# A two-layer hybrid diffusion step on one core: the start of the slots woven into the last features, RWKV factors taken off GpSimd

## The chip, the core and the metric

The kernel runs on 1 core of one Trainium2 chip. The metric is the device time of one execution in microseconds (us). TensorE does the matrix products, VectorE, ScalarE and GpSimd the elementwise work, and SyncE (SP) issues every DMA. All arithmetic is fp32; most products run as three passes over operands split into a high and a low part ("mm3").

## What is computed

Two layers work on 1152 tokens: 1024 latent ones and 128 of a prompt. Cut to what matters here, a layer of the reference is:

```python
u = layer_norm(x) * (1.0 + scale) + shift                    # adaLN from the conditioning
r, k, v, g, cq, ckv, kr, gm, xl, gl = split_in(u @ w_in)     # "features": columns of w_in
y_rw, S_fin = rwkv_branch(u, r, k, v, g, S0, l, P)           # scan over tokens, both directions
y_mla = block_attention(qn, qr, kn, kr_all, vv) * silu(gm)   # 8 heads, softmax over 1152 keys
y_lru, h_fin = lru_branch(xl, gl, h0, l, P)
x = layer_norm(ALPHA * x + gate * (concat(y_rw, y_mla, y_lru) @ w_out))

# a step of the RWKV scan, per head of 64
sa = S @ (-kk_t);  S = S * w_t + sa (x) (kk_t * a_t) + v_t (x) k_t;  y = S @ r_t
```

The latent tokens read the prompt's cached context, the prompt's tokens only themselves, so their attention is over 128 keys (no more than one tile).

## The kernel before

**Stages of a layer.** First come values, rope keys and latents of all tokens (token tiles of 128), then the queries, then 16 "features": column tiles of 128 of the input projection, each over three blocks of 384 tokens (24 matmuls a block). The loop over `n_` walks them in `order`. Weights of three features are loaded and split at a time. Other work is hung on the loop: a piece of the next adaLN per feature (`adaln_piece`), the LRU scan (`lru_piece`, features 3 to 8) and the RWKV factors (`rwkv_tile`, `RW_AT`: two token tiles at each of features 9 to 12 and the last at 13, nine in all). The last three features are taken by token block instead: feature step 13 does block 0 of all three, 14 block 1, 15 block 2.

**RWKV factors.** For each tile of 128 tokens and each direction d, `rwkv_tile` makes four factors from the summed log decay Lc: z = exp(Lc - lw) times the negated normalised key, r = exp(Lc) times the receptance, b and k from exp(-Lc). `gtt` is GpSimd's tensor_tensor, `vtt`, `vts` and `vstt` are VectorE's, `act` and `sca_` ScalarE's. The normalised key `nkk` lies in a tile of tag `mxb`, of which there is one; the results lie in tags `abz` and `ls`, two each, and go to DRAM (`zr_d`, `bk_d`).

**Values and slots.** `value(i)` makes the attention values of key tile i (ten of them, the tenth is the prompt's). After that the layer runs 48 slots, three for each unit of one head and 512 queries. A slot has named blocks (A0, G, A1, B, C, S) in which queued work is hung: queries are loaded (`load_q`) and split (`split_q`, the subtraction on GpSimd) some slots ahead, the row maxima of the scores are found (`max_q` for four query tiles over 1024 keys, `max_last` for the rest, `max_rows` puts them into the query), heads' keys are made (`keys`), and the RWKV chunks are taken through their products (`win_load`, `win_products`, `win_transposes`), the inversion of a triangular matrix (`inv_load`, `inv_blocks16` on GpSimd, `inv_store`) and the scan. Work of negative slots is what the slots begin from: the first head's keys, the first units' maxima, the first chunks' products. All maxima use the one PSUM tile of tag `b`.

**The prompt's attention** (two units `ups` of four heads) is done before the slots: `prompt_keys`, `max_last`, `max_rows`, `scores`, `values`, `sums`, then `finish` (reciprocals of the sums, through DRAM and back to be spread over partitions) and `gate`. Both take their queries in `qs_`, the tiles that the first units use too.

**Order.** The Tile framework orders the instructions of each engine by priority (the order in which they are written) and readiness, and gives out the tiles. The prompt and the negative slots are written after all values, in a block with a raised priority:

```python
        with tc.high_priority(offset=tc.cur_priority - p_late):
            value(9)
            ...
            for g, u in enumerate(ups):
                prompt_keys(g)
                max_last(u)
                ...
            for slot in range(min(s for s, _ in todo), 0):
                for b in ("A0", "G", "A1", "B", "C", "S"):
                    run(slot, b)
```

Large tiles come from tag `t`, ten buffers: the normalised tokens `Ub` (six, two for each block), weights, keys, the values V0 and V1, and the tiles `sets`, `s3`, `s4`, `s5` of the RWKV chunks (`s5` holds the inversion's X and U_).

## Time and profile before

| | |
|---|---|
| three runs, median (lowest, highest) | 2005.73 us (2003.27, 2010.9) |
| profiled execution | 2003.78 us, span of its instructions 2001.9 us |
| TensorE busy / mean granted clock | 1815.0 us / 0.944 |
| VectorE, ScalarE, GpSimd busy | 1202.3, 924.4, 684.7 us |

In the views, PE is TensorE, PEld its weight loads, DVE VectorE, ACT ScalarE, POOL GpSimd. "busy, mean ns" of a group is the summed time and the mean of one instruction; "idle before <- releaser" is the time in which the engine stood idle just before it, and what it waited for. PEclk is the granted TensorE clock as a share of 2.4 GHz. L121, L116 are the helpers through which the matmuls and the VectorE and ScalarE instructions are issued. Stages are at these times: RWKV factors begin in layer 0 at 336.57 us and in layer 1 at 1342.10, slot 0's scores at 511.47 and 1491.04.

### The profile page before, as it was taken

To read this page: it belongs to the slowest core of one execution; us is meant where nothing else is said; L and a number is where in the kernel's file an instruction comes from. 1 tells how busy PE (TensorE), PEld (TensorE's weight loads), DVE (VectorE), ACT (ScalarE), POOL (GpSimd) and SP (SyncE) were. 2 spreads that over 40 slices of the span, in tenths; PEclk is the share of its full clock that TensorE was granted. 3 is DMA by queue.
4 is the path that set the end of the run, shared out by engine and by line. 5 is a ranking of instruction groups with operands and counts; after the bars stand their busy time and mean duration, and the time that the engine had idled before them with its cause. 6 is when DMAs were issued, how large, how long until landed. Compare 5 with 4: busy or idle time off the path is not lost.

```text
span 2001.9 us, 47694 instructions
## 1 busy us (share of the span) xinstructions
PE 1815.0 (91%) x18494; PEld 1527.9 (76%) x18494; DVE 1202.3 (60%) x2472; ACT 924.4 (46%) x2069; POOL 684.7 (34%) x1159
## 2 busy tenths in 40 slices
PE   6899998888899999994998999997779999998898
PEld 4798887786687787763877999997657778776686
DVE  6744445883456565764778443569735565666476
ACT  2533566442454554553235426675325455555421
POOL 1410011461434434322545100126424444441353
PEclk8999999887899999997998999998869999999999
DMA  8334444653335444437443252435533443334542
GB/s 298 109 96 153 131 122 139 208 179 107 90 95 126 115 114 103 118 107 221 151 138 111 93 173 87 121 113 173 172 84 66 108 93 99 89 89 141 154 155 85
DMA packets 346242, 256.34 MB, mean 128 GB/s; under 512 B 116968, under 2 KB 285600, under 8 KB 344992
## 3 DMA queue, kind: packets, MB, share of 16 engines
q1 hardware_dynamic: 346016, 253.30, 43.3%
q8 instruction: 145, 2.38, 0.5%
q14 instruction: 81, 0.66, 0.1%
HBM read 174.38 MB, written 78.78 MB: 126 GB/s over the span
## 4 chain that ended last, share of the span: by engine, by line
PE 68%; DVE 12%; DMA 10%; ACT 3%; issue 3%; SPq 2%; POOL 1%; DVEq 0%; ACTq 0%; POOLq 0%
PE ps_a L121 46%; PE ps_pv L121 7%; PE ps_b L121 5%; PE ps_rw L121 4%; PE ps_cx L121 4%; DVE ls L116 4%; DVE rw L116 3%; DVE sm L116 2%; DVE t L116 1%; DMA mxb<-inv_d 1%; DMA kp<-in_wout_dram 1%; DMA t<-zr_d 1%; DMA ls<-l_d 1%; DMA l_d<-sm 1%; ACT t L116 1%
## 5 line engine op out<-in xcount | busy, mean ns | idle before, releaser
L121 PE MATMUL ps_a<-t,t 128*128 128x384 f32 (+3 forms) x6048 | 708.8, 296 | 20.7 <-DVE t L116 5.4
L121 PEld LDWEIGHTS ps_a<-t,t 128*128 128x128 f32 (+1 forms) x6048 | 650.9, 167 | 48.5 <-ACT pe L116 14.1
L116 DVE TENSOR_REDUCE sm<-ps_b 128x1 f32<-128x1024 f32 (+1 forms) x164 | 181.3, 1106 | 123.4 <-PE ps_b L121 122.1
L121 PE MATMUL ps_a<-q,t 128*128 128x512 f32 (+1 forms) x912 | 233.6, 402 | 8.9 <-DVE ep L116 4.0
L116 ACT ACTIVATE pe<-ps_a 128x512 f32<-128x512 f32 (+1 forms) x296 | 168.3, 575 | 137.1 <-PE ps_a L121 125.3
L121 PEld LDWEIGHTS ps_a<-q,t 128*128 128x128 f32 x912 | 172.7, 198 | 54.1 <-issue 11.5
L121 PE MATMUL ps_a<-t,q 128*128 128x512 f32 (+1 forms) x544 | 161.6, 381 | 0.0
L116 DVE TENSOR_TENSOR t<-kp,t 128x512 fp32r<-128x512 f32 (+2 forms) x128 | 86.5, 704 | 87.9 <-ACT t L116 87.6
L121 PE MATMUL ps_a<-t,kp 128*128 128x512 f32 (+1 forms) x304 | 118.0, 390 | 22.7 <-DVE kp L116 22.7
L121 PE MATMUL ps_b<-t,q 96*128 96x512 f32 (+1 forms) x400 | 116.2, 388 | 22.9 <-DVE sm L116 17.0
L116 ACT CAST t<-kp 128x512 fp32r<-128x512 f32 (+2 forms) x128 | 73.3, 601 | 119.8 <-DMA kp<-in_wft_dram 47.7
L121 PE MATMUL ps_pv<-pe,t 128*64 128x256 f32 x928 | 125.3, 391 | 0.0
L121 PEld LDWEIGHTS ps_a<-t,q 128*128 128x128 f32 x544 | 100.0, 188 | 21.9
L520 POOL TENSOR_TENSOR rw<-rw 128x512 f32<-128x512 f32 (+1 forms) x24 | 20.0, 832 | 263.8 <-ACT rw L116 172.8
L121 PEld LDWEIGHTS ps_b<-t,q 96*128 96x128 f32 x400 | 67.5, 201 | 50.0 <-DVE sm L116 23.3
L855 POOL TENSOR_TENSOR t<-t 64x15 f32<-64x15 f32 (+2 forms) x270 | 72.4, 268 | 76.9 <-DVE t L116 43.0
L116 DVE TENSOR_TENSOR t<-ps_a,t 128x512 f32<-128x512 f32 (+2 forms) x106 | 65.5, 625 | 40.3 <-ACT t L116 33.5
L157 POOL TENSOR_TENSOR sm<-sm,nhalf 128x1 f32<-128x1 f32 (+1 forms) x54 | 34.3, 637 | 155.5 <-DVE sm L116 150.1
L121 PEld LDWEIGHTS ps_pv<-pe,t 128*64 128x64 f32 x928 | 59.8, 137 | 34.2 <-issue 8.6
L121 PEld LDWEIGHTS ps_a<-t,kp 128*128 128x128 f32 x304 | 58.3, 192 | 35.4 <-DVE kp L116 23.5
L1066 POOL TENSOR_TENSOR q<-q,q 96x512 fp32r<-96x512 f32 x36 | 47.3, 1314 | 100.6 <-ACT q L116 99.2
L121 PEld LDWEIGHTS ps_cx<-t,t 128*64 128x64 f32 (+1 forms) x1752 | 65.5, 138 | 20.3 <-ACT t L116 8.9
(258 smaller groups left out, 3253.7 us busy)
## 6 DMA issues: line engine op xcount, KB each, us to landing
kp<-in_wft_dram SPq DMA_DIRECT2D x64, 256.0 KB
kp<-in_wmod_dram SPq DMA_DIRECT2D x64, 256.0 KB
rw<-in_x_dram SPq DMA_DIRECT2D x36, 256.0 KB
gate_d<-pe SPq DMA_DIRECT2D x48, 192.0 KB
bk_d<-ls SPq DMA_DIRECT2D x36, 256.0 KB
zr_d<-abz SPq DMA_DIRECT2D x36, 256.0 KB
t<-bk_d SPq DMA_DIRECT2D x18, 512.0 KB
t<-zr_d SPq DMA_DIRECT2D x36, 256.0 KB
```

Source lines behind the costliest of these rows:

```text
L116: return lambda *a, **k: in_line(getattr(self.eng, op)(*a, **k))
L121: return in_line(nc.tensor.matmul(*a, **k))
L157: gtt(out, t[:, :n], nhalf.to_broadcast([128, n]), op=POW)
L520: gtt(q_, a_, a_, op=MUL)
L855: gtt(tv, U_[0:64, 0:t, t:t + 1].to_broadcast([64, t, n]), X[0:64, t:t + 1, t:16].to_broadcast([64, t, n]), op=MUL)
L1066: gtt(qo[0:96], ql, qh[0:96], op=SUB)
```

## The change

In `rwkv_tile` the three GpSimd instructions of each direction go. The exponential of Lc - lw is no longer computed: exp(Lc) of the neighbouring token is the same number, so z is r shifted by one token times nkk, on VectorE, and the chunk's end token is a copy of nkk on ScalarE. The product for r moves to VectorE. From VectorE to ScalarE go the scaling of the decay, the copy of the chunks' last decay (wcs) and k's scale and offset.

The loop over features becomes a generator `features`, and its last two steps are run piece by piece between the negative slots. `value(0)` to `value(8)` no longer stand together, but between the prompt's steps. The prompt's queries get a large tile of their own (`promptq`, tag `t`). The second prompt unit is finished and gated in slot 0. The two adaLN pieces of those feature steps are kept back for them. No arithmetic of the weave changes.

```diff
@@ -573,7 +573,7 @@
                         b_ = 4 * a + 2 * d + f
                         act(t_[:, d, f], ps[:, a, f], AF.Tanh, bias=hv[:, b_:b_ + 1], scale=0.5)
             lw_, Lc = tw, W("rw2", D4)
-            vec_.tensor_scalar(fl(lw_), fl(tw), LWS, LWS, op0=MUL, op1=ADD)
+            act(fl(lw_), fl(tw), AF.Copy, bias=LWS, scale=LWS)
             f1 = lambda t, d: t[:, d].rearrange("p f t -> p (f t)")
             vec_.tensor_tensor_scan(f1(Lc, 0), rst, f1(lw_, 0), 0.0, op0=MUL, op1=ADD)
             vec_.tensor_tensor_scan(f1(Lc, 1)[:, ::-1], rst, f1(lw_, 1)[:, ::-1], 0.0, op0=MUL, op1=ADD)
@@ -582,18 +582,19 @@
             for d in range(2):
                 zr, bk = W("abz", [128, 2, 2, 2, 64]), W("ls", [128, 2, 2, 2, 64])
                 z, r, b, k = (t[:, :, :, x].rearrange("p f c t -> p (f c) t") for t in (zr, bk) for x in range(2))
-                gtt(z, ch(Lc[:, d]), ch(lw_[:, d]), op=SUB)
-                act(z, z, AF.Exp)
                 act(r, ch(Lc[:, d]), AF.Exp)
                 act(b, ch(Lc[:, d]), AF.Exp, scale=-1.0)
                 if d == 0:
-                    vec_.tensor_copy(wcs[:, 0, q0:q0 + 2].rearrange("p q f -> p f q"), zr[:, :, :, 1, 63])
+                    sca_.copy(wcs[:, 0, q0:q0 + 2].rearrange("p q f -> p f q"), zr[:, :, :, 1, 63])
                 else:
-                    vec_.tensor_copy(wcs[:, 1, q1:q1 + 2].rearrange("p q f -> p f q"), zr[:, :, ::-1, 1, 0])
-                gtt(z, z, ch(nkk), op=MUL)
-                gtt(r, r, ch(r_), op=MUL)
+                    sca_.copy(wcs[:, 1, q1:q1 + 2].rearrange("p q f -> p f q"), zr[:, :, ::-1, 1, 0])
+
+                at_, of_, end_ = (slice(1, 64), slice(0, 63), 0) if d == 0 else (slice(0, 63), slice(1, 64), 63)
+                sca_.copy(z[:, :, end_], ch(nkk)[:, :, end_])
+                vtt(z[:, :, at_], r[:, :, of_], ch(nkk)[:, :, at_], op=MUL)
+                vtt(r, r, ch(r_), op=MUL)
                 for f in range(2):
-                    vts(bk[:, f, :, 1], ta[:, d, f].rearrange("p (c t) -> p c t", c=2), kah[:, f:f + 1], omk[:, f:f + 1], op0=MUL, op1=ADD)
+                    act(bk[:, f, :, 1], ta[:, d, f].rearrange("p (c t) -> p c t", c=2), AF.Identity, bias=omk[:, f:f + 1], scale=kah[:, f:f + 1])
                 vtt(k, k, ch(k_), op=MUL)
                 vtt(k, k, b, op=MUL)
                 vstt(ta[:, d], ta[:, d], 1.0, nkk, ADD, MUL)
@@ -688,9 +689,8 @@
                 vstt(e, e, 1.0, ps, ADD, MUL)
                 dma(gate_d[gi, :, bs], e)
 
-        for n_ in range(NFT):
-            if n_ == NFT - 2:
-                p_late = tc.cur_priority
+        def features(n_):
+            nonlocal ada_todo, wh, wl
             t = order[n_]
             if n_ % 3 == 1 or n_ == 0:
                 ts = order[n_:n_ + (3 if n_ else 1)]
@@ -704,6 +704,7 @@
                 rope_keys()
             for j in range(3):
                 feature(*((n_, j) if n_ < NFT - 3 else (NFT - 3 + j, n_ - (NFT - 3))))
+                yield
             if t == FT_R + 1:
                 bt_ = T("smr", [128, 2, NTILE, 2])
                 vec_.tensor_scalar(bt_.rearrange("p e i f -> p (i f) e"), bps[:, :36].rearrange("p (a e) -> p a e", e=2), 0.5, None, op0=MUL)
@@ -728,6 +729,9 @@
                 lru_piece(*divmod(n_ - LRU_AT, 3))
             for i in RW_AT.get(n_, ()):
                 rwkv_tile(i)
+        for n_ in range(NFT - 2):
+            for _ in features(n_):
+                pass
         dma(lru_out[l], lru_fin)
         if dbg.get("stop") == "win":
             continue
@@ -745,15 +749,13 @@
             mm3(ps, [(ckvh[:, ks], ckvl[:, ks], wv[0], wv[1])])
             (vec_.tensor_copy if i % 2 else sca_.copy)(val(i), ps)
 
-        for i in range(9):
-            value(i)
-
 
         lnx = sb.tile([128, 2, 2, 64], F32, name=f"lnx{l}", tag="lnx", bufs=1)
         for eo in range(2):
             dma(lnx[64 * eo:64 * eo + 64], lnx_in[l, eo:eo + 1].rearrange("o a b c -> o (a b c)").to_broadcast([64, 256]))
         vec_.tensor_scalar(lnx, lnx, 0.5, None, op0=MUL)
         N_d = dram([2, 4, 2, 65, 64], "N_d", 2)
+        promptq = W("t", [128, 4, 512], F32R)
         sets = [T("t", [128, 3072]) for _ in range(3)]
         s3, s4, s5 = (T("t", [128, 3072]) for _ in range(3))
         U8 = [128, 2, 4, 64]
@@ -1049,7 +1051,7 @@
 
         def load_q(u):
             h, q0 = u["h"], u["q0"]
-            qh, qo = u["qh"], u["qo"] = qs_[u["i"] % 3]
+            qh, qo = u["qh"], u["qo"] = u["qs"] if "qs" in u else qs_[u["i"] % 3]
             ql = qo[0:96].bitcast(F32)
             qr = qr_d[128 * (h // 4):128 * (h // 4) + 128].rearrange("(m h) t -> m h t", h=4)
             if q0 < NS:
@@ -1207,11 +1209,11 @@
             if s0 + 5 < nslot:
                 at(s0 + 4, "G", finish, u)
                 at(s0 + 5, "G", gate, u)
-        for k_, todo_ in enumerate(ada_todo):
+        for k_, todo_ in enumerate(ada_todo[2:]):
             ada_ = adaln_piece(*todo_)
             at(3 * k_ + 1, "S", next, ada_)
             at(3 * k_ + 2, "A1", next, ada_, None)
-        ada_todo = []
+        ada_todo = ada_todo[:2]
         CH = 7
         for i in range(9):
             c = CH + 4 * i
@@ -1244,24 +1246,63 @@
                     tail.append(gn)
 
 
-        with tc.high_priority(offset=tc.cur_priority - p_late):
-            value(9)
-            ups = [dict(h=4 * g, q0=NS, i=g, pe=[]) for g in range(2)]
-            for u in ups:
-                load_q(u)
-                split_q(u)
-            for g, u in enumerate(ups):
-                prompt_keys(g)
-                max_last(u)
-                max_rows(u)
-                scores(u, 0)
-                values(u)
-                sums(u)
-                finish(u)
-                gate(u)
-            for slot in range(min(s for s, _ in todo), 0):
-                for b in ("A0", "G", "A1", "B", "C", "S"):
-                    run(slot, b)
+        def early(slot):
+            for b in ("A0", "G", "A1", "B", "C", "S"):
+                run(slot, b)
+
+        assert min(s for s, _ in todo) == -6
+        last_features = (x for n_ in (NFT - 2, NFT - 1) for x in features(n_))
+
+        def more(n):
+            for _ in range(n):
+                next(last_features, None)
+
+        def prompt(u):
+            values(u)
+            sums(u)
+
+        ups = [dict(h=4 * g, q0=NS, i=g, pe=[]) for g in range(2)]
+        for u, t_ in zip(ups, (promptq[:, 0:2], promptq[:, 2:4])):
+            u["qs"] = [t_[:, e] for e in range(2)]
+        more(2)
+        early(-6)
+        more(2)
+        early(-5)
+        more(1)
+        more(2)
+        for u in ups:
+            for t_ in u["qs"]:
+                nc.gpsimd.memset(t_[96:128].bitcast(F32), 0.0)
+            load_q(u)
+            split_q(u)
+        early(-4)
+        value(0)
+        prompt_keys(0)
+        early(-3)
+        value(1)
+        max_last(ups[0])
+        value(2)
+        max_rows(ups[0])
+        early(-2)
+        value(9)
+        value(3)
+        scores(ups[0], 0)
+        prompt_keys(1)
+        value(4)
+        max_last(ups[1])
+        prompt(ups[0])
+        value(5)
+        early(-1)
+        max_rows(ups[1])
+        value(6)
+        scores(ups[1], 0)
+        value(7)
+        value(8)
+        finish(ups[0])
+        gate(ups[0])
+        prompt(ups[1])
+        todo.setdefault((0, "C"), []).insert(0, (finish, (ups[1],)))
+        at(0, "S", gate, ups[1])
         line.update(on=True, last={})
         for slot in range(nslot):
             u = us[slot // 3]
```

## Rows read from the trace of the kernel before

**Rows 1.** The page: busy time by engine, and TensorE's busy tenths in 40 slices.

```profile
PE 1815.0 (91%) x18494; PEld 1527.9 (76%) x18494; DVE 1202.3 (60%) x2472; ACT 924.4 (46%) x2069; POOL 684.7 (34%) x1159
...
PE   6899998888899999994998999997779999998898
```

**Rows 2.** Busy time by stretch: PE, PEld, DVE, ACT, POOL, granted clock, DMA share, GB/s.

```profile
336.57:458.10 121.53, 99.19 (x645) 93.00 (x644) 100.25 (x219) 55.50 (x163) 61.20 (x74) 0.89 0.54 179
458.10:511.47 53.37, 38.56 (x279) 28.78 (x279) 18.65 (x29) 14.40 (x36) 13.35 (x33) 0.67 0.43 120
1342.10:1438.50 96.40, 76.69 (x411) 71.21 (x412) 89.98 (x195) 45.76 (x142) 58.70 (x69) 0.86 0.47 158
1438.50:1491.04 52.54, 37.84 (x272) 28.11 (x272) 18.61 (x29) 13.85 (x35) 13.33 (x33) 0.66 0.49 137
```

**Rows 3.** Waits from 337 to 446 us: total, times, longest.

```profile
POOL abz L585 <- DVE rw L116: 24.0, 5, 9.1
...
PE ps_a L121 <- DVE ep L116: 21.5, 5, 5.9
```

**Rows 4.** Groups of VectorE from 337 to 446 us, shapes kept apart.

```profile
L116 DVE TENSOR_SCALAR ls<-rw,hv 128x128 f32<-128x128 f32 x36 | 17.0, 534 | 7.1 <-ACT rw L116 5.5 <-DMA bk_d<-ls 1.5
L116 DVE TENSOR_TENSOR_SCAN rw<-kc,rw 128x256 f32<-128x256 f32 x18 | 12.5, 735 | 0.1
...
L116 DVE COPY wcs<-abz 128x4 f32<-128x4 f32 x18 | 7.1, 397 | 0.4 <-ACT abz L116 0.4
...
L116 DVE TENSOR_SCALAR rw<-rw 128x512 f32<-128x512 f32 x9 | 4.8, 539 | 0.2 <-ACT rw L116 0.2
```

**Rows 5.** VectorE by tile, 337 to 446 us: shortest, median and longest, ns.

```profile
L116 DVE TENSOR_SCALAR ls<-rw,hv x36: 318/348/1915, 338.7 to 445.2; 128x128 f32<-128x128 f32 x36
L116 DVE TENSOR_TENSOR ls<-ls,rw x18: 407/418/958, 339.4 to 445.6; 128x256 f32<-128x256 f32 x18
...
L116 DVE TENSOR_TENSOR_SCAN rw<-kc,rw x18: 660/682/1722, 340.9 to 440.3; 128x256 f32<-128x256 f32 x18
```

**Rows 6.** Timelines of VectorE and GpSimd, 405 to 419 us: start, us.

```profile
413.86 2.61 DVE L116 TENSOR_SCALAR ls<-rw,hv 128x128 f32<-128x128 f32 x2
...
411.36 3.64 POOL L1066 TENSOR_TENSOR q<-q,q 96x512 fp32r<-96x512 f32 x2 [0.78 <-DMA q<-qr_d]
```

**Rows 7.** ScalarE: groups (337 to 446 us, whole span) and one tile.

```profile
L116 ACT ACTIVATE abz<-abz 128x256 f32<-128x256 f32 x18 | 7.3, 416 | 3.4 <-POOL abz L585 3.3
L116 ACT CAST t<-kp 128x512 fp32r<-128x512 f32 x6 | 3.8, 626 | 9.1 <-DMA kp<-in_wft_dram 9.1
...
L116 ACT ACTIVATE sp<-sp 128x4 f32<-128x4 f32 x2 | 0.4, 206 | 7.7 <-DVE sp L116 7.7
...
L116 ACT ACTIVATE rw<-ps_rw,modT x68: 434/457/517, 36.3 to 1093.5; 128x128 f32<-128x128 f32 x68
```

**Rows 8.** Timelines of SP and VectorE in layer 1: the tile mxb.

```profile
1405.72 0.58 SPq L559 DMA_DIRECT2D mxb<-inv_d  x1
...
1410.75 1.10 DVE L116 SCALAR_TENSOR_TENSOR mxb<-rw,vec,mxb 128x128 f32<-128x128 f32 x2
...
1414.92 0.58 SPq L559 DMA_DIRECT2D mxb<-inv_d  x1
```

**Rows 9.** Timelines of TensorE and VectorE before slot 0 of layer 0.

```profile
503.97 1.11 PE L121 MATMUL ps_b<-t,q 96*128 96x128 f32 x4 [4.51 <-DVE sm L116]
...
507.92 1.22 PE L121 MATMUL ps_b<-t,q 96*128 96x512 f32 x2 [1.27 <-ACT q L116]
510.46 1.22 PE L121 MATMUL ps_b<-t,q 96*128 96x512 f32 x2 [1.32 <-DVE sm L116]
...
502.35 0.42 DVE L116 TENSOR_TENSOR ep<-ep,ls 128x256 f32<-128x256 f32 x1 [4.17 <-DMA ls<-l_d]
```

**Rows 10.** Timelines of GpSimd and ScalarE: the first inversion's end, its copy.

```profile
514.42 0.21 POOL L856 TENSOR_TENSOR t<-t 64x15 f32<-64x15 f32 x1
...
526.97 1.04 ACT L116 COPY t<-t 32x256 f32<-32x256 f32 x2
```

## The prediction

> **What bounds the kernel now.** I read the profile page first, then the busy time of each engine in chosen stretches, then waits and instruction groups inside them, and last the timelines. The page says that TensorE is busy for 91% of the span, and its slices say where the rest is lost: in the long rows of nines, most of them slots, there is little to win, and a slice of 4 to 8 has holes [rows 1]. The view by stretch [rows 2] shows the stretches of this change. Layer 0 and layer 1 each have two such stretches. The first, A, runs from the first RWKV tile's matmuls to the last feature or factor (336.57 to 458.10 and 1342.10 to 1438.50). The second, B, runs from there to the first scores of slot 0 (up to 511.47 and 1491.04). An estimate of TensorE's work in a stretch at its upper clock level of 2.4 GHz is busy time by granted clock: 99.19 x 0.89 = 88.3 and 38.56 x 0.67 = 25.8 us in layer 0, 76.69 x 0.86 = 66.0 and 37.84 x 0.66 = 25.0 us in layer 1. So 205 us of work takes 323.8 us, and 119 us is what this change can win at the very most.
>
> In A the engine at its limit is VectorE: 100.25 of 121.53 us and 89.98 of 96.40 us busy [rows 2]. What is queued behind its factors waits: in layer 0 TensorE waits 21.5 us in five times for the copy of an adaLN row on VectorE, and GpSimd waits 24.0 us for the cumulated decay [rows 3]. VectorE's time is not all its own. A tensor_scalar of 128x128 takes 0.318 us alone, 0.534 us on average and up to 1.915 us; the scan 0.660 us alone and up to 1.722 us [rows 4, 5]. The long ones lie under GpSimd's instructions: two tensor_scalars take 2.61 us where GpSimd splits a query until 415.00 [rows 6]. In B no engine is full. TensorE has 38 us of busy time at a clock of 0.66, between round trips through VectorE, ScalarE and DMA [rows 2, 9].
>
> **The change, RWKV factors.** Per layer there are 9 tiles with two directions each.
>
> VectorE loses 36 tensor_scalars (17.0 us), 9 scalings of the decay (4.8) and 18 copies of wcs (7.1), 28.9 us together [rows 4]. It gains 36 multiplications of at most 128x256 from GpSimd, at 0.407 us alone (0.48 is the bound from the same form under GpSimd's load, which is what goes): 14.7 to 17.3 us [rows 5]. What stays loses its slow cases; for the 18 scans that is 18 x (0.735 - 0.660) = 1.4 us [rows 4, 5]. The other groups that stay have their longest case at about 0.95 us against 0.41 alone, as the one shown, and I put the whole relief at 10 us, between 0 and 15. So layer 0's A needs 100.25 - 28.9 + 14.7 - 10 = 76 us of VectorE, and layer 1's 89.98 - 28.9 + 14.7 - 10 = 66 us [rows 2]. It is no longer the longest.
>
> ScalarE loses 18 exponentials (7.3 us) and gains per tile one 128x512 Copy (at most the 0.626 of a cast), four pieces of a few columns (0.21 each, nearest row) and four Identities with two pointers of 128x128 (0.46) [rows 7]. That is 0.63 + 0.84 + 1.84 = 3.3 us per tile, 30 per layer, net +22: 55.5 to 78 us in layer 0, 45.8 to 68 us in layer 1. It is the second engine now, still below TensorE's 88 and near its 66. For the four Identities the Trainium skill speaks against the change: "ScalarE: Activation LUTs" (Rules for kernel authors) wants additions and multiplications on VectorE, and its cost section gives 186 + 2 x 93 + 0.833 x 128 = 479 ns for such an instruction, an estimate from that page that the row's 434 to 517 ns bears out [rows 7]. By that rule's preference the four would cost 4 x 0.32 us on an undisturbed VectorE against 4 x 0.46 us here, 5 us per layer to ScalarE's account; the sum is the same as long as TensorE is the longer.
>
> GpSimd loses all 54 of its multiplications and subtractions here and keeps the key fills. "SBUF — State Buffer" of the Trainium skill (Who interferes with whom) calls the pair of ports that VectorE and GpSimd share an exclusive lock; by it nearly all of GpSimd's time in A would come back to VectorE, more than the 10 us that I take, and VectorE would still not be the bound.
>
> What then limits A? One loop is not throughput: the tile that holds the normalised key (mxb) exists once. In layer 1's even part it is reloaded at 1405.72 and again at 1414.92, 9.20 us a tile; VectorE's first use comes at 1410.75, 5.03 us after the issue [rows 8]. The load stays. Its users become the two products (0.6 alone), z's multiplication and the product with a in both directions, four instructions at 0.41, with others between. That gives 5.0 + 0.6 + 1.6 = 7.2 us at best and 9.2 as now at worst; I take 8.1. Nine tiles and the first one's lead of 5 us make 78 us, which is layer 1's new A: VectorE, ScalarE and TensorE all lie below. In layer 0 TensorE's 88.3 plus 1.5 for the nine key matmuls woven in is longer; with a tenth for the adaLN waits that remain, 98 us. So A gains 121.5 - 98 = 23.5 us (between 0 and 32) and 96.4 - 78 = 18.4 us (between 0 and 29).
>
> **The change, the weave.** Before, prompt and first query share query tiles, and the order is values, prompt 0, prompt 1, first maxima one after the other. Now the prompt has tiles of its own, keys of head 0 and the split of the first query lie among the last features, and the rest is dealt between ten values. Nothing is removed: the work of B stays 25 us, less 1.5. Its other chain is the one PSUM tile of two banks: a first maximum every 2.54 us (507.92 to 510.46), and 3.95 us from the last maxima's matmuls to the next use (503.97 to 507.92) [rows 9]. Five of the first and three of the second make 24.6 us. The two run beside each other, so B lies between 25 us and the 53 of now; with in-order engines that hand on to each other I take 32. That is a gain of 53.4 - 32 = 21.4 and 52.5 - 32 = 20.5 us.
>
> Moved DMAs: the loads of prompt and first query go ahead of the last stores on SP's queue; they are few, and SP is not held there. The second prompt's finish and gate move into slot 0, in its last two blocks. The gate waits for a round trip of two DMAs; today VectorE waits 4.17 us for such a one [rows 9]. Behind it on VectorE stand slot 1's maxima, and TensorE waits for their PSUM. I charge 3 us per layer.
>
> The eleventh large tile on ten buffers may hold back the tile of the inversion until prompt 1 has its scores. The inversion ends on GpSimd at 514.63 and ScalarE copies it at 526.97 [rows 10], so 12.3 us of delay are covered; I charge nothing.
>
> **The sum.** Profiled execution 2003.8 us (span 2001.9). Layer 0: 23.5 + 21.4 = 44.9; layer 1: 18.4 + 20.5 = 38.9; back 2 x 3. 2003.8 - 83.8 + 6 = 1926 us. The median of the runs, 2005.7, lies 1.9 above the profiled one, so 1928 us.
>
> **The rivals.**
> - *A gains nothing.* The place of GpSimd's waits is taken by ScalarE: its copy of z's end waits for the mxb load, and the features' evacuations are queued behind it on ScalarE; or the loop stays at 9.2 us. For it: the load's 5 us are untouched [rows 8], and ScalarE gets 22 us more. Against it: VectorE is nearly full now [rows 2]. Then 21.4 + 20.5 - 6 = 36 us are won: 1970.
> - *B gains nothing,* because the single PSUM tile and the round trips set it and not the order. Against it: 24.6 us of that chain in 53. Then 23.5 + 18.4 - 6 = 36: also 1970.
> - *TensorE is filled,* at 94% of the time in all four stretches: 205 / 0.94 = 218 instead of 324, 106 won, 6 back: 1906, or below.
> - *Slower.* The woven stretches have TensorE with small holes throughout, and the granted clock falls in all of A, as it did in B (0.67 [rows 2]). The 114 us of layer 0's work then take 114 / clock. The point where it decides is 114 / 174.9 = 0.65 in layer 0 and 91 / 148.9 = 0.61 in layer 1. At 0.6 they take 190 and 152 us, 18 us more: 2024. Against it: in A the clock is 0.86 to 0.89 with more holes than I expect afterwards.
> - *No change:* what is won returns in the slots, where the later inversion would need to be over 12.3 us late in each layer and cost some 40 us there. I see nothing that large.
>
> **How the numbers follow.** Forecast (both parts, 1910 to 1955) 0.58; one part alone (1955 to 1985) 0.22; TensorE filled (below 1910) 0.09; no change 0.05; slower 0.06. 0.5% of the time, 10 us, is what a measurement here can tell from no change. Faster 0.89, same 0.05, slower 0.06. The forecast, most of one part alone and half of the filled case give 1898 to 1980 as the range for 8 in 10.
>
> **What would show it.** A: VectorE's tensor forms at their lone durations (0.41 and 0.66 us), about 75 and 66 us busy, the mxb loads about 8 us apart, and layer 0's adaLN waits under 10 us. B: under 35 us from the last feature to slot 0, granted clock near 0.9. Wrong would be: mxb loads still 9 us apart, ScalarE waiting for mxb, B above 45 us, or a VectorE wait for the gate in slot 0 well above 5 us.

## The result, and the profile after

The changed kernel takes 1948.45 us (median of 4 runs, 1945.55 to 1964.21) against 2004.86 us before (4 runs beside them): ratio 0.9729, with a 95% interval of 0.9673 to 0.9785. The prediction was 1928 us in a range of 1898 to 1980. The profiled execution went from 2003.78 to 1949.72 us, 54.1 us less where 78 were predicted. Cut at the events that the prediction used, it divides like this (slot 0 is the start of its first scores; the inverse norms are the store of `inv_d` in layer 1):

| part | before, us | after, us | gain | predicted |
|---|---|---|---|---|
| layer 0, A | 121.5 | 114.4 | 7.1 | 23.5 |
| layer 0, B | 53.4 | 30.5 | 22.9 | 21.4 |
| layer 0's slot 0 to layer 1's inverse norms | 784.1 | 785.6 | -1.5 | -3 |
| layer 1, inverse norms to slot 0 (A and B) | 195.4 | 162.0 | 33.4 | 38.9 |
| layer 1, slot 0 to the end | 510.9 | 518.6 | -7.7 | -3 |

(The first RWKV matmul of layer 0 came 0.2 us later.) So layer 0's B came out as predicted, its A gained less than a third, and the slots gave back half as much again as charged.

The page after, the busy line and TensorE's tenths:

```profile
PE 1798.9 (92%) x18494; PEld 1511.6 (78%) x18494; DVE 1155.1 (59%) x2418; ACT 954.3 (49%) x2195; POOL 596.7 (31%) x1059
...
PE   7899999888999999994998999999889999998898
```

The busy times by stretch, columns as in [rows 2]: A and B of layer 0, then layer 1 from the inverse norms to the last feature and from there to slot 0. In layer 1 the first RWKV matmul now stands among earlier features (at 1291.36), so the inverse norms are the fairer mark there.

```profile
336.78:451.19 114.41, 102.28 (x657) 93.64 (x656) 79.96 (x198) 74.06 (x231) 19.56 (x24) 0.93 0.64 210
451.19:481.72 30.53, 24.00 (x265) 18.51 (x266) 13.57 (x22) 12.28 (x31) 12.56 (x37) 0.98 0.37 100
1267.30:1390.58 123.28, 117.39 (x678) 109.20 (x676) 85.42 (x198) 96.26 (x257) 18.78 (x24) 0.97 0.55 177
1390.58:1429.34 38.76, 30.71 (x268) 23.04 (x268) 23.05 (x38) 14.81 (x40) 17.77 (x47) 0.82 0.38 104
```

The same two stretches of layer 1 in the kernel before:

```profile
1295.60:1428.38 132.78, 120.41 (x667) 113.31 (x666) 106.29 (x220) 79.69 (x194) 59.76 (x70) 0.92 0.45 145
1428.38:1491.04 62.66, 40.58 (x279) 29.58 (x278) 26.44 (x45) 15.91 (x40) 19.14 (x44) 0.66 0.45 130
```

VectorE is no longer the full engine: 80 of 114 us where it had 100 of 122. TensorE is now the nearest to its limit, 117.39 of 123.28 us in layer 1. In B the granted clock went from 0.67 and 0.66 to 0.98 and 0.82 with nearly as many products (279 in each layer before, 265 and 268 now).

The waits of the changed kernel from 337 to 446 us, which answer to [rows 3]:

```profile
PE ps_a L121 <- DVE ep L116: 8.2, 4, 2.9
DVE mxb L116 <- DMA mxb<-inv_d: 7.2, 5, 2.2
ACT abz L116 <- DVE mxb L116: 5.9, 5, 1.6
```

VectorE's forms by tile in that stretch (shortest, median and longest, ns), which answer to [rows 5]:

```profile
L116 DVE TENSOR_TENSOR ls<-ls,rw x18: 393/419/427, 341.7 to 438.1; 128x256 f32<-128x256 f32 x18
...
L116 DVE TENSOR_TENSOR_SCAN rw<-kc,rw x18: 660/672/1409, 342.4 to 422.2; 128x256 f32<-128x256 f32 x18
...
L116 DVE TENSOR_TENSOR abz<-abz,rw x18: 407/420/440, 346.5 to 429.6; 128x256 f32<-128x256 f32 x18
```

GpSimd's wait in `rwkv_tile` is gone with its instructions, the products of 128x256 sit at 0.42 us with almost no slow case, and TensorE's wait for the adaLN row fell from 21.5 to 8.2 us. VectorE's wait for the load of the one `mxb` tile has grown from 2.0 to 7.2 us, and ScalarE now waits behind it.

The last view shows what the slots gave back: VectorE's timeline at slot 0 of layer 1 (start, duration, instruction, idle time ahead of it).

```profile
1426.58 0.18 DVE L116 RECIPROCAL sm<-sm 128x4 f32<-128x4 f32 x1 [3.74 <-DMA sm<-l_d]
...
1432.16 0.42 DVE L116 TENSOR_TENSOR ep<-ep,ls 128x256 f32<-128x256 f32 x1 [3.69 <-DMA ls<-l_d]
1432.50 1.22 DVE L116 TENSOR_REDUCE sm<-ps_b 128x1 f32<-128x1024 f32 x1
...
1437.77 0.18 DVE L116 RECIPROCAL sm<-sm 128x4 f32<-128x4 f32 x1 [2.01 <-DMA sm<-l_d]
...
1443.12 1.02 DVE L116 TENSOR_TENSOR ep<-ep,ls 128x256 f32<-128x256 f32 x1 [3.81 <-DMA ls<-l_d]
```

TensorE's waits there, in its own timeline:

```profile
1433.77 0.73 PE L121 MATMUL ps_b<-t,q 96*128 96x512 f32 x2 [2.20 <-DVE sm L116]
...
1445.33 0.66 PE L121 MATMUL ps_b<-t,q 96*128 96x128 f32 x4 [4.14 <-DVE sm L116]
```

Both prompt units' gates (`ep<-ep,ls`) fall within the first two slots, the first at 1432, the second at 1443, and each is the end of two round trips through DRAM: the sums out and back for the reciprocal, the reciprocals out and back for the gate. VectorE stands still for 13.3 us in these four places, and the maximum of the next scores (`sm<-ps_b`) waits behind each gate, with TensorE behind that, 2.20 and 4.14 us. From slot 0's first exponential on ScalarE to slot 2's, which is 15.0 us in layer 0 and 15.1 in layer 1 before, it is now 20.4 and 23.1: 5.3 and 8.1 us lost within two slots.

### The profile page after: what moved, and what is told of

It reads as the page before. It is cut to its first block, busy times and chain, and to the rows that moved or that the text cites. A ratio compares the mean times of both kernels' runs of the same rounds, so it can differ in the third digit from the quotient of the medians.

```text
span 1947.9 us, 47608 instructions
## 1 busy us (share of the span) xinstructions
PE 1798.9 (92%) x18494; PEld 1511.6 (78%) x18494; DVE 1155.1 (59%) x2418; ACT 954.3 (49%) x2195; POOL 596.7 (31%) x1059
## 4 chain that ended last, share of the span: by engine, by line
PE 56%; DMA 9%; DVE 7%; ACT 3%; issue 2%; SPq 1%; POOL 1%; DVEq 0%; ACTq 0%; POOLq 0%
PE ps_a L121 37%; PE ps_pv L121 6%; PE ps_b L121 5%; PE ps_cx L121 4%; PE ps_rw L121 4%; DVE rw L116 2%; DVE sm L116 2%; DMA ls<-l_d 1%; DVE t L116 1%; DMA l_d<-sm 1%; DMA t<-zr_d 1%; DMA kp<-in_wout_dram 1%; ACT rw L116 1%; DVE ls L116 1%; DMA mxb<-inv_d 1%
## 5 line engine op out<-in xcount | busy, mean ns | idle before, releaser
L121 PE MATMUL ps_a<-t,t 128*128 128x384 f32 (+4 forms) x6096 | 713.7, 296 | 25.2 <-DVE t L116 6.4
L121 PE MATMUL ps_a<-q,t 128*128 128x512 f32 x864 | 220.2, 399 | 3.3 <-DVE ep L116 3.0
L121 PEld LDWEIGHTS ps_a<-q,t 128*128 128x128 f32 x864 | 160.3, 189 | 46.2 <-issue 7.3
L116 DVE TENSOR_TENSOR t<-kp,t 128x512 fp32r<-128x512 f32 (+2 forms) x128 | 88.3, 717 | 82.5 <-ACT t L116 81.9
L121 PE MATMUL ps_b<-t,q 96*128 96x512 f32 (+1 forms) x384 | 108.5, 377 | 19.5 <-DVE sm L116 17.0
L121 PEld LDWEIGHTS ps_b<-t,q 96*128 96x128 f32 x384 | 62.6, 193 | 43.1 <-DVE sm L116 21.6
L857 POOL TENSOR_TENSOR t<-t 64x15 f32<-64x15 f32 (+2 forms) x270 | 72.8, 270 | 64.3 <-DVE t L116 30.1
L116 DVE TENSOR_TENSOR t<-ps_a,t 128x512 f32<-128x512 f32 (+2 forms) x106 | 65.3, 624 | 27.0 <-ACT t L116 20.3
L858 POOL TENSOR_TENSOR t<-t 64x15 f32<-64x15 f32 (+2 forms) x270 | 74.0, 274 | 20.3
```

The lines of the kernel that those rows point to most:

```text
L116: return lambda *a, **k: in_line(getattr(self.eng, op)(*a, **k))
L121: return in_line(nc.tensor.matmul(*a, **k))
L857: gtt(tv, U_[0:64, 0:t, t:t + 1].to_broadcast([64, t, n]), X[0:64, t:t + 1, t:16].to_broadcast([64, t, n]), op=MUL)
L858: gtt(X[0:64, 0:t, t:16], X[0:64, 0:t, t:16], tv, op=ADD)
```

## Experiments

Ratios are to the kernel before, run beside each on the same chip, with their 95% intervals.

### The two parts apart

`factors_alone` is the kernel before with the new `rwkv_tile`; `weave_alone` is the changed kernel with the old one. Their edits are the first two and the remaining hunks of the diff.

> The kernel before with the new RWKV factors alone, nothing woven. By the prediction's sum stretch A gains 23.5 us in layer 0 and 18.4 in layer 1, so about 1963 us. By the reading of the changed kernel's trace (layer 0's A shrank by 7 us with some 5 us of the woven work taken in; layer 1 gained 9.5 us between the inverse norms and the last feature) the factors give about 12 + 10 us, so about 1983 us. Either way the two VectorE waits behind GpSimd are gone: the scan near 0.70 us, and TensorE's waits for the adaLN row in layer 0's A fall from 21.5 us to about 8.

> The changed kernel with the RWKV factors as before (GpSimd's three instructions, VectorE's scalings and copies), so only the weave. If the two parts add up, B alone gives 21 us a layer less about 4 us in the slots: about 1970 us, and its gain plus that of the factors alone is the 56 us of both. The rival: the woven keys and first maxima are queued behind a VectorE that is full in A, and wait there; then A grows by over 5 us a layer and the weave alone gives under 30 us, above 1975, with the two gains adding up to less than that of both.

Measured: factors alone 1984.34 us, 0.9893 (0.9872 to 0.9914); weave alone 1979.08 us, 0.9869 (0.9844 to 0.9893). The first is what the changed kernel's trace led to expect (1983), the second is 9 us above the sum of the expectation (1970). The product of the two ratios, 0.9763, lies in the interval of both together (0.9673 to 0.9785), but by the medians the parts give 20.3 and 25.6 us, 45.9 against 56.4. So the times alone can't tell whether the parts add up or fall some 10 us short. The spans of the profiled executions lose 24.8 and 27.6 us, 52.4 against 54.0. Factors alone, A and B of layer 0, then layer 1 from the inverse norms, cut at the last feature:

```profile
337.61:448.28 110.67, 98.14 (x642) 91.57 (x642) 76.96 (x192) 71.38 (x226) 12.67 (x16) 0.92 0.60 197
448.28:505.92 57.64, 38.20 (x280) 28.56 (x281) 18.78 (x29) 14.29 (x36) 14.62 (x37) 0.67 0.42 111
1285.14:1403.23 118.09, 114.60 (x668) 108.07 (x667) 83.65 (x194) 92.75 (x249) 12.67 (x18) 0.97 0.49 161
1403.23:1468.05 64.82, 41.66 (x277) 29.75 (x277) 25.71 (x44) 17.98 (x49) 19.18 (x45) 0.66 0.46 130
```

Weave alone, the same:

```profile
338.13:465.45 127.32, 102.41 (x656) 94.58 (x655) 102.39 (x224) 57.62 (x168) 65.50 (x82) 0.89 0.58 189
465.45:496.10 30.65, 24.20 (x266) 18.79 (x267) 14.70 (x23) 12.23 (x31) 12.41 (x37) 0.93 0.43 107
1281.31:1424.20 142.89, 123.28 (x678) 114.79 (x677) 113.71 (x232) 83.07 (x201) 69.95 (x84) 0.89 0.48 154
1424.20:1461.05 36.85, 29.12 (x269) 22.07 (x268) 18.97 (x31) 12.69 (x33) 14.22 (x41) 0.86 0.40 109
```

With the kernel before and the changed one this is a square, in us:

| | layer 0 A | layer 0 B | layer 1 A | layer 1 B |
|---|---|---|---|---|
| neither | 121.5 | 53.4 | 132.8 | 62.7 |
| factors alone | 110.7 | 57.6 | 118.1 | 64.8 |
| weave alone | 127.3 | 30.7 | 142.9 | 36.9 |
| both | 114.4 | 30.5 | 123.3 | 38.8 |

In these stretches the parts do not add up: A and B of both layers shrink by 19.1 us with the factors, by 32.6 with the weave and by 63.4 with both, 11.6 more than the sum. Outside them the factors alone gain 5.7 us, the weave alone loses 5.0 and both lose 9.4, mostly in the slots. That the whole spans nearly add up is a balance of the two.

The factors take 10.9 us from layer 0's A without the weave and 12.9 with it, 14.7 and 19.6 from layer 1's. They give 2 to 4 us back in B when B is not woven. The weave takes 23 to 27 us from B, in whichever company, and costs A 5.8 us (3.7 with the new factors) and 10.1 us (5.2). The rival of the second expectation came true in its signs: the weave alone makes A grow by over 5 us in both layers, gives under 30 us and stays above 1975. Woven work beside a full VectorE costs A 1.6 and 1.9 times what it costs beside a freed one.

### The gates of the prompt

```diff
         finish(ups[0])
-        gate(ups[0])
         prompt(ups[1])
+        todo.setdefault((0, "G"), []).insert(0, (gate, (ups[0],)))
         todo.setdefault((0, "C"), []).insert(0, (finish, (ups[1],)))
-        at(0, "S", gate, ups[1])
+        todo.setdefault((1, "G"), []).insert(0, (gate, (ups[1],)))
```

> The changed kernel, with the gate of the first prompt unit moved from before slot 0 into slot 0, and the gate of the second from the end of slot 0 into slot 1. If VectorE's waits for the round trips (4.9 us before slot 0, 2.8 us in it) are what the prediction charged 3 us a layer for, TensorE's waits of 4.1 and 1.9 us behind them go and the time falls by 6 to 10 us over both layers, to about 1940. If TensorE waits there for something else (the one PSUM tile of the maxima), the time stays within 2 us of the changed kernel's.

Measured: 1934.2 us, 0.9644 (0.9618 to 0.9671), 14 us below the changed kernel, more than the 6 to 10 expected. VectorE at the same place in layer 1:

```profile
1422.90 0.18 DVE L116 RECIPROCAL sm<-sm 128x4 f32<-128x4 f32 x1 [3.55 <-DMA sm<-l_d]
...
1426.04 1.23 DVE L116 TENSOR_REDUCE sm<-ps_b 128x1 f32<-128x1024 f32 x1 [1.26 <-PE ps_b L121]
1428.31 0.42 DVE L116 TENSOR_TENSOR ep<-ep,ls 128x256 f32<-128x256 f32 x1 [1.04 <-DMA ls<-l_d]
...
1434.78 1.21 DVE L116 TENSOR_REDUCE sm<-ps_b 128x1 f32<-128x1024 f32 x1
1438.49 0.81 DVE L116 TENSOR_TENSOR ep<-ep,ls 128x256 f32<-128x256 f32 x1 [2.50 <-DMA ls<-l_d]
```

Each gate now stands one row maximum later in VectorE's queue, and its wait is shorter. The reciprocals still wait, 3.55 and 3.45 us, so VectorE stands for 10.5 us in the four places; but TensorE waits nowhere in those slots for over 1 us. The first two slots take 15.4 us in layer 0 and 16.1 in layer 1, 12.0 us less than in the changed kernel and 0.4 and 1.0 us more than before. So what these slots gave back was the gates. That the profiled execution gains just as much (1949.72 to 1937.61) is in part chance: layer 0's later slots took back 4.5 of the 5.0 us that its first two gained, slot 0 there came 3.2 us earlier, and layer 1 gained 8.6 us from slot 0 on.

### The adaLN rows in layer 0's A

In `ada_split` the second half of each piece comes one feature later; `ada_gate` is that with the later gates. `ada_early` (with the later gates) takes the pieces of features 8 to 13 two at a time in features 0 to 5. `row_act` (with the later gates) copies the row on ScalarE.

The edit of `ada_split`:

```diff
-            for todo in ada_todo[:ka]:
-                for _ in adaln_piece(*todo):
-                    pass
+            for a_ in ada_open:
+                next(a_, None)
+            ada_open[:] = [adaln_piece(*todo) for todo in ada_todo[:ka]]
+            for a_ in ada_open:
+                next(a_)
+                if n_ == NFT - 1:
+                    next(a_, None)
```

of `ada_early`:

```diff
-            ka = 2 if n_ < 0 else 1
+            ka = 2 if n_ < 6 else 1 if n_ < 8 or n_ >= NFT - 2 else 0
```

and of `row_act`:

```diff
-        vec_.tensor_copy(row, ps[:, :cw])
+        (vec_.tensor_copy if cw == 256 else sca_.copy)(row, ps[:, :cw])
```

> The changed kernel, with the second half of each adaLN piece one feature step later than its first, so that the copy of its row has a whole feature's matmuls to pass VectorE's queue. If TensorE's waits for that row (8.2 us) and the half clock behind them (about 3, 2 and 2 us in the three feature blocks that follow) set the length of A in layer 0, layer 0 gains 10 to 15 us and the time is about 1936. If the loop over the one mxb tile or ScalarE's 74 us set it, the wait moves there and the time is within 4 us of the changed kernel's 1948. Layer 1 has no such pieces in A and stays.

> The later gates and the divided adaLN pieces together. With the gates out of the way the profiled kernel with divided pieces alone had its slot 0 of layer 0 5.9 us earlier than the changed kernel (475.9 against 481.7 us), but was held longer in slots 0 and 1 (7.8 us over before, against 5.3). If those gates swallowed the gain, this one is 4 to 7 us below the kernel with later gates alone (1934), at about 1929. If the pieces are worth nothing, it is at 1934.

> The later gates, and the adaLN pieces of features 8 to 13 taken two at a time in features 0 to 5, ahead of the RWKV factors; none is left in A until its last two features. If the adaLN rows queued behind VectorE's factors, and TensorE's half clock after each such wait, hold layer 0's A, slot 0 of layer 0 comes 10 us or more earlier than with the later gates alone (478.6 us), less what the pieces now cost before A (1 us each of TensorE, and a wait of their own where VectorE has the LRU scan); the time is about 1924 to 1928. If A is held by the normalised key's loop or by ScalarE, A stays at about 112 us and the time is 1934 or above.

> The later gates, and the copy of an adaLN row (128x128) from PSUM on ScalarE in place of VectorE. If TensorE's wait for it (8.7 us in four times in A with the later gates alone) is VectorE's queue, it falls under 4 us, with the half clock behind it, and slot 0 of layer 0 comes some 8 us before 478.6: about 1926 us. If ScalarE's queue (73 us busy in 110) holds the row as long, the wait only gets ScalarE's name and the time stays at 1934 within 3.

Measured: `ada_split` 1949.12 us, 0.9728 (0.9702 to 0.9755), `ada_gate` 1931.69, 0.9640 (0.9621 to 0.9660): no difference from the changed kernel and from the later gates that could be told. `ada_early` 1944.79, 0.9710 (0.9685 to 0.9734), and `row_act` 1954.8, 0.9762 (0.9738 to 0.9787), are slower than the later gates, `row_act` by 20 us where at most 3 were expected. TensorE's waits from 336 to 452 us in `ada_split`:

```profile
PE ps_a L121 <- DVE modT L116: 4.9, 3, 2.7
PE ps_b L121 <- ACT t L116: 4.4, 1, 4.4
```

in `ada_early`:

```profile
PE ps_cx L121 <- ACT rw L116: 4.3, 3, 3.2
PE ps_b L121 <- ACT t L116: 3.3, 1, 3.3
PE ps_a L121 <- DVE pe L116: 1.5, 2, 1.2
PE ps_a L121 <- DVE ep L116: 0.9, 1, 0.9
```

and in `row_act` from 336 to 464 us:

```profile
PE ps_a L121 <- ACT ep L116: 10.8, 5, 3.4
```

My theory that the time hangs on the row's place in VectorE's queue in layer 0's A fell. When that wait went, others came: with divided pieces the bias added to the second half (`modT`) and a wait for ScalarE, with the copy on ScalarE the same row in ScalarE's queue. A itself does get shorter: from 113.0 to 106.4 us in `ada_split` (to the end of the last feature's matmuls), and from the first tile's key load to the last feature from 138.8 us with the later gates to 129.0 with `ada_early`. But what lies ahead of A gets longer: the inverse norms go out at 316.0 us in `ada_split` (308.6 in the changed kernel) and at 324.67 in `ada_early` (310.09 with the later gates). For the six pieces of `ada_early` that is 9.8 us less in A, 1.6 a piece, and 14.6 us more ahead of it, 2.4 a piece.

`row_act` is no clean test of A, since its edit moves 32 row copies in the whole program. Of the 19.2 us that its profiled execution is longer than that of the later gates, 7.2 come ahead of the inverse norms of layer 0, 3.9 from there to slot 0, and the rest in later stages, 7.9 of it from slot 0 on in the two layers.

### The one tile of the normalised key, and ScalarE's share

Both with the later gates: `nkk_gate` puts the key into a buffer of `rw2`, `ident_gate` puts k's scale and offset back on VectorE.

The edit of `nkk_gate`:

```diff
-            rk, nkk = W("rw2", D4), W("mxb", [128, 2, 128])
+            rk, nkk = W("rw2", D4), W("rw2", [128, 2, 128])
```

and of `ident_gate`:

```diff
-                    act(bk[:, f, :, 1], ta[:, d, f].rearrange("p (c t) -> p c t", c=2), AF.Identity, bias=omk[:, f:f + 1], scale=kah[:, f:f + 1])
+                    vts(bk[:, f, :, 1], ta[:, d, f].rearrange("p (c t) -> p c t", c=2), kah[:, f:f + 1], omk[:, f:f + 1], op0=MUL, op1=ADD)
```

> The later gates, and the normalised key in a buffer of the tag rw2 (eight buffers) in place of the one mxb tile, so that its load no longer waits for the tile before. If the mxb loop (loads 9.7 us apart in layer 1) and VectorE's waits for that load (7 to 10 us in each layer's A) hold A, A shrinks by 5 to 10 us a layer, to about 1920 to 1925. If A is held by TensorE in layer 1 (busy 117 of 123 us from the inverse norms to the last feature) and by the adaLN rows in layer 0, the time stays at 1934 within 4.

> The later gates, and k's scale and offset (36 instructions of 128x128 a layer) back from ScalarE on VectorE, at 0.32 us there against 0.44 to 0.50 here. If ScalarE (74 us busy in 114 of layer 0's A, 79 in 99 of layer 1's) is what delays the evacuations, A shrinks by some 5 us a layer: about 1925. If VectorE's in-order queue is (it carries the adaLN row and the mxb users), A grows by up to 36 x 0.32 = 12 us a layer, to 1940 or more. If neither, 1934 within 4.

Measured: `nkk_gate` 1927.91 us, 0.9620 (0.9600 to 0.9640), between the two expectations; its interval meets that of the later gates. The traces tell more than the times. SP's loads of the key in layer 1, in the changed kernel:

```profile
1357.73 1.25 SPq L559 DMA_DIRECT2D mxb<-inv_d  x2
1367.77 0.58 SPq L559 DMA_DIRECT2D mxb<-inv_d  x1
...
1377.98 0.58 SPq L559 DMA_DIRECT2D mxb<-inv_d  x1
...
1387.85 1.23 SPq L559 DMA_DIRECT2D mxb<-inv_d  x2
```

and in `nkk_gate`:

```profile
1344.01 1.24 SPq L559 DMA_DIRECT2D rw<-inv_d  x2
1352.71 1.91 SPq L559 DMA_DIRECT2D rw<-inv_d  x2
1362.24 1.23 SPq L559 DMA_DIRECT2D rw<-inv_d  x2
1371.53 0.58 SPq L559 DMA_DIRECT2D rw<-inv_d  x1
```

From the second tile's load to the ninth's it is 9.75 us a tile in the changed kernel (1319.63 to 1387.85, seven steps), 9.76 with the later gates, 8.67 in `nkk_gate` (1310.82 to 1371.53), and layer 1's stretch from the inverse norms to slot 0 falls from 162.1 us with the later gates to 155.9. It falls in the two other pairs that differ by this buffer too, as the next section shows. So there the one tile did cost time. It is not the loop alone that sets its pace: with the same one tile and nothing woven in, `factors_alone` has 8.86 us a tile (1337.42 to 1399.44). In layer 0 A did not gain (115.9 us against 111.6), so there the tile is not what holds it.

`ident_gate` 1941.18 us, 0.9688 (0.9672 to 0.9704): 7 us slower than the later gates, as by the theory that VectorE's queue counts (1940 or more). But A did not grow by 12 us a layer: from the inverse norms to slot 0 layer 0 takes 2.0 us more than with the later gates, layer 1 6.6. TensorE's wait for the adaLN row in layer 0 grows from 8.7 to 12.5 us; the wait for the key's load does not grow, it falls from 15.7 to 5.8 us in both layers.

### The best of it

`ada_gate_nkk` joins later gates, divided pieces and the key in `rw2`; `ada_early_nkk` has the early pieces instead of the divided ones; `row_act_ada_nkk` is the first with the row's copy on ScalarE.

> Later gates, divided adaLN pieces and the normalised key in a buffer of rw2. Alone over the later gates (1934.2) the pieces gave 2.5 us and the key's buffer 6.3; if they add up, 1925. The key's buffer gained in layer 1's A and lost 5 us in layer 0's, where the adaLN rows are; if that loss was the rows' waits, the divided pieces take it away and the time is about 1922. If the two only reorder the same work, 1928 to 1932.

> Later gates, adaLN pieces ahead of A and the normalised key in a buffer of rw2. If layer 0's A is held by the rows and layer 1's start by the single key tile, both gains add: about 1918 to 1922. If the pieces ahead of A cost as much as they save in it, 1928 as with the key's buffer and later gates alone.

> The fastest so far (later gates, divided adaLN pieces, the normalised key in rw2: 1921) with the row's copy on ScalarE as well. With the pieces divided the row has a feature's time anyway, and what TensorE still waits for (6.8 us in four times) is the bias added to the second half's product on VectorE, which stays. So 1921 within 3, and this is the best that these edits give; if the row's copy on VectorE still counted, 1915 or less.

Measured: `ada_gate_nkk` 1921.06 us, 0.9587 (0.9559 to 0.9616); `ada_early_nkk` 1923.78, 0.9613 (0.9586 to 0.9639); `row_act_ada_nkk` 1933.58, 0.9656 (0.9639 to 0.9674). Divided pieces, which gave nothing that could be told by themselves, go with the key's buffer, to 1921 as expected (1922). Slot 0 of layer 0 starts at 474.5 us with both, at 474.3 with the divided pieces alone, at 483.5 with the buffer alone and at 478.6 with neither: the 5 us that the buffer lost there are gone. Layer 1 from the inverse norms to slot 0 takes 158.7 us with both and 163.1 without the buffer; with early pieces 154.6 and 164.4. By the medians the buffer is worth 6.3 us with undivided pieces, 10.6 with divided and 21.0 with early ones, and only the first of these is not clear of the noise.

With later gates, divided pieces and the key in `rw2` the kernel is 27 us below the changed one and 4.1% below before; `ada_early_nkk` can't be told from it. The row on ScalarE cost some 12 us here too, where I had expected nothing. Why it costs this much, no run shows.

## Why the prediction was right, point by point

- **What bounds A, and what the factors free.** Right. Layer 0's VectorE was to need 76 us; factors alone it needs 76.96. The relief that I took as 10 us is what is left over: 100.25 - 28.9 + 14.7 - 76.96 = 9.1. ScalarE was to need 78 and needs 71 to 74. GpSimd lost 48.5 us in that run (61.2 to 12.67), and VectorE got back 9.1 of these 48.5 us. "SBUF — State Buffer" of the Trainium skill (Who interferes with whom) calls the shared ports an exclusive lock. From that I had concluded that nearly all of GpSimd's time would come back. The section does not say that: by it an instruction of VectorE contends only with two inputs in SBUF or in a two-port mode, and the engine that issues second is the one blocked. No run here tells how much of the 9.1 us was the lock.
- **Layer 0's A, "TensorE's work and a tenth": the step that failed.** It was mis-sized, by 16 us of the 24 missing. Three terms make the 16.4. The tenth, 8.2 us, stood for the adaLN waits alone, and these did come to 8.2 us in the changed kernel; but TensorE idled 12.1 us, 3.9 of them on other waits. For the clock the sum had nothing: at 0.93 over 102.28 busy us it costs 7.2 us. And the work itself is 102.28 x 0.93 = 95.1 us where I had 89.8; since factors alone it is 98.14 x 0.92 = 90 against 88.3, most of this is woven work, which adds 3.7 us to A where I had counted 1.5. The prediction also took the row's wait to be a matter of a full VectorE. With VectorE at 70% it still cost 11.7 us factors alone, and the experiments show that other waits come where it goes. What sets the length of layer 0's A stays open.
- **Layer 1's A, the mxb loop at 8.1 us a tile.** The loop costs time, but it is not the bound that I made it, and its size was wrong: 9.75 us a tile, above the 9.2 that I called the worst. Two of the prediction's own signs of being wrong came, loads still over 9 us apart and ScalarE waiting for the key (5.9 us in five times in layer 0). I had read the 9.20 from one step; over seven steps it was 10.65 before (1350.17 to 1424.75), so the loop did get faster. Without the weave it takes 8.86, with more buffers 8.67. The prediction had TensorE well below this loop; from the inverse norms to the last feature it is busy 95% of the time, and that leaves little to win there. That layer 1 as a whole still gave 33.4 of 38.9 us is thus in part luck.
- **B at 32 us.** Right in layer 0: 30.5, and `weave_alone` shows that it is the order alone that does it (30.7). The two chains do run beside each other. In layer 1 it is 38.8 from the last feature at a clock of 0.82, over the 35 and under the 0.9 that the prediction named as signs. There the last store of factors leaves at 1409.80, 19 us behind the last feature; in layer 0 it leaves 11 us ahead of it. That this is why, no run shows.
- **Slots, 3 us a layer for the gate.** The mechanism was right, the size was not: 5.3 and 8.1 us within two slots, 9.1 us net. I priced one wait of a gate (4.17 us [rows 9]). There are two gates, both within reach of slot 0, each with a second round trip ahead of it in which VectorE waits before the reciprocal.
- **Nothing for the inversion.** Right: with the gates moved, the stretches from slot 0 on are within about 1 us of those before in both layers.
- **The rivals.** A did gain, by 7 us in layer 0 and 9.5 in layer 1 with woven work inside, so the first is wrong as a whole, though both its reasons showed: ScalarE waits for the key, and the loop stays over 9 us a tile. The second is refuted by `weave_alone`. TensorE is not filled: by busy time and clock it has 118.6 us of work in the 144.9 of layer 0's A and B, 82%. For the slower one the clock would have had to fall to 0.65; A's rose from 0.89 to 0.93.
- **k's scale and offset on ScalarE.** "ScalarE: Activation LUTs" of the Trainium skill (Rules for kernel authors) prefers VectorE for them. For the single instruction the trace agrees: 0.34 us on VectorE in `ident_gate`, 0.49 on ScalarE with the later gates (medians). For this kernel's time it does not: back on VectorE they cost 7 us, and TensorE's wait for the adaLN row behind VectorE's queue grows by 3.8 us in layer 0. What cost most of it, in layer 1, no run singles out.

## What to carry to other kernels

When a full engine is relieved, the waits behind its in-order queue shrink but do not go to nothing (here from 21.5 to 8.2 us): price every wait that remains, and add what TensorE's clock loses behind the waits (7.2 us beside 12.1 here). A step that ends in round trips through DRAM and is moved into a dense loop needs its consumer queued later; moving two such lines behind one more row maximum each was worth 14 us, a quarter of what the whole change brought. Two parts whose times nearly add up can still act on each other: look at the stretches and not only at the sum. And when a move looks like a gain in one stretch, read the stretch ahead of it too: pieces taken out of A shortened A by 10 us and lengthened what lies before it by 15.

## What the runs showed of the hardware

Behind the longer waits in A, TensorE's clock fell, and that cost more than half as much again. In the changed kernel TensorE is busy 1.08 of 4.02 us before 368.50 while it waits for a row; the features that follow run at a granted clock of 0.73, 50 matmuls in 11.31 us. At full clock 51 instructions of the same stream take 8.74 us (48 of each are the features' matmuls of 128x384), so a wait of 2.9 us was followed by a loss of 2.6. The same at 391.36 (0.68) behind a wait of 2.80 us, while after the short waits around 435 the clock stays full:

```profile
364.48:368.50 4.02, 1.08 (x19) 0.81 (x19) 3.82 (x11) 4.02 (x17) 0.00 (x0) 0.91 0.56 186
368.50:379.81 11.31, 11.31 (x50) 11.06 (x50) 9.63 (x24) 6.81 (x19) 0.00 (x0) 0.73 0.82 271
1273.35:1282.09 8.74, 8.74 (x51) 8.50 (x50) 2.62 (x4) 5.96 (x9) 1.04 (x1) 1.00 0.15 44
391.36:396.75 5.39, 5.39 (x24) 5.14 (x23) 4.67 (x12) 4.69 (x15) 2.53 (x3) 0.68 0.94 306
434.77:449.75 14.98, 14.24 (x93) 13.36 (x92) 5.71 (x11) 2.30 (x6) 0.04 (x1) 1.00 0.36 111
```

In TensorE's timeline 21 matmuls take 5.46 us behind the wait of 2.80, and 23 of the same shape 4.24 us behind one of 1.18, so the first lost some 1.6 us:

```profile
391.11 0.38 PE L121 MATMUL ps_a<-kc,ep 128*128 128x2 f32 x2 [2.80 <-DVE ep L116]
391.36 5.46 PE L121 MATMUL ps_a<-t,t 128*128 128x384 f32 x21
...
411.87 0.38 PE L121 MATMUL ps_a<-kc,ep 128*128 128x2 f32 x2 [1.18 <-DVE ep L116]
412.11 4.24 PE L121 MATMUL ps_a<-t,t 128*128 128x384 f32 x23
```

0.73 and 0.68 are means between the two levels, 1.2 and 2.4 GHz: part of each stretch at the lower, the rest at the upper. What besides the wait lowered it there, no run here tells apart.
